# Scores of a chunked gated scan on four column tiles, collected compactly with one masked copy a level

## The chip, the core and the metric

The kernel runs on one core of a Trainium2 chip. The metric is the device time of one execution in microseconds; less is better. The profile comes from one execution. Its engines are called PE (TensorE, matmuls), PEld (the weight loads of TensorE, which overlap the matmuls), DVE (VectorE), ACT (ScalarE), POOL (GpSimd) and SP (SyncE, which issues the DMAs).

## What is computed

One layer of a trunk over 2048 latent positions of width 1024, with a prefix of 256 positions, all in float32. The input is normalised, modulated and projected (w_in); the projections feed a bidirectional gated scan with four heads of 128 channels and a spatial gate with four heads; then come an output projection and a gated MLP with a 3x3 convolution. The change is inside the scan's products within a chunk. In the reference they are:

```
b = jnp.cumsum(gc, axis=2)
diff = b[:, :, :, None, :] - b[:, :, None, :, :]
decay = jnp.where(mask, jnp.exp(jnp.where(mask, diff, 0.0)), 0.0)
scores = jnp.einsum('bhtk,bhsk,bhtsk->bhts', qc, kc, decay)
o = o_inter + jnp.einsum('bhts,bhsv->bhtv', scores, vc)
```

The score of a position t with a position s sums, over the 128 channels, q at t, k at s and the product of the forget gates between them. One such sum runs forwards in time and one backwards.

## The kernel before

The sequence is worked in two halves of 1024 positions (TH), a half in 8 chunks (NCH) of 128 positions (P). In the first stage, function run_banks sends the projections of all heads to PE, bank by bank: a bank is 512 positions of 128 output columns, 24 matmuls of 512 columns in a split precision (xh, xl and whi, wlo; tile pj, three banks). Into this stream two queues of generators put their steps: hg_q the scans of the heads, bg_q the background work (among it w_down_ops, line 1024). A step comes when the planner's clock T.t (class Tensor, line 57), which adds an assumed time for each matmul, has passed the wait that the last step yielded; the clock is looked at between the matmuls of a bank (slot). The wait counts from behind the matmuls of the step that yields it. Before the last four banks open_wo drains both queues.

A head's scan is the generator hg (line 795), which runs eight times: four heads in each of two halves. Layout: positions of a chunk by positions of a chunk, tile sc of 128 partitions (s) by 8 chunks by 128 (t). Its steps are:

- the diagonal: kd is q times the sum of both directions' k; its sums over the 128 channels are needed in every row, so a matmul with a matrix of ones takes them. kd is split in kh and kl (fp32r, an ACT cast at line 802 and a DVE subtraction at line 804), and column_sums (line 790) multiplies both by the 128 ones, 512 columns at a time. ACT copies the result over all of sc (line 813).
- level 1: the products kn of neighbours, split in knh and knl (lines 825, 826) and summed in the same way; a DVE masked copy puts them in sc (line 856).
- levels B = 2, 4, 8, 16, 32, 64 (LV): within a block of 2B positions, each half of B is scored against the other. For each chunk two float32 matmuls of 64 weights (from K) and 64 columns (from Q) fill two squares of 64 by 64, in two PSUM banks (tag sc, two of them); the two stand on different halves of the array's columns, since their outputs go to PSUM partitions 0 to 63 and 64 to 127. Up to level 32, four DVE masked copies (line 860) put in sc what belongs to the level; level 64 is copied by ACT (lines 852, 853).
- behind each level, Q is multiplied by the level's gate products (level_update, line 518), K likewise into another tile (level_keys: DVE and POOL at line 595, ACT copies at line 598, at level 64 lines 587 and 588), and the gate products are merged (next_tot, line 525). Then the step yields 4.2.
- behind the levels: K is transposed (kt), the states of the chunks are made and chained (fs and bs_, line 781), and sc, Q and the states give the output. The output gates (o_gate, line 771) run later.

On-chip tiles are named by tags; tiles of the same tag share their slots, and a new one waits until the old one was read for the last time. kd lies in Q, kh and sc in slot S, kl and knl in T1, knh in on. The slot fs holds the states and, in the second half, the gate sgb of the scan that was deferred. Except where pin stands, the framework may order the instructions of an engine anew.

Of the kernel before, what the change touches and what calls it, by code (L numbers as in the profile page):

```python
# [17 lines left out]

P = 128
HB = 64  # L20
D = 1024
NK = D // P
SEQ = 2048
# [28 lines left out]
def view(t, off, dims):  # L52

    return bass.AP(t.tensor, t.offset + off, [list(t.ap[0])] + [list(d) for d in dims])


class Tensor:
# [5 lines left out]
    def matmul(self, out, lhsT, rhs, **kw):  # L63
        n = 1
        for _, count in rhs.ap[1:]:
            n *= count
        m = lhsT.ap[-1][1] / P
        self.t += n / 2400 + 0.0135 if rhs.dtype == F32R else 2 * max(0.112 * m, n / 1200 + 0.005)
        return self.engine.matmul(out, lhsT, rhs, **kw)  # L69

    def transpose(self, out, in_, identity):
# [16 lines left out]
def tile_trunk(ctx, tc, x, c, cx, c_ctx, w_ada, b_ada, norm_mix, norm_ffn, w_in, hg_norm, sgu_g, sgu_b,  # L88
# [105 lines left out]
    with es1:  # L194
# [5 lines left out]
        wa = [p1.tile([P, NK, TH], F32, tag=t, name="wa", align_bytes=AL) for t in ("xl", "xh")]  # L200
        wsT = pm.tile([P, NH, P], F32, name="wsT")
        rh = pm.tile([P, NH, P], F32, name="rh")
        msk = pm.tile([P, 8, P], U8, name="msk")
        hf = [pm.tile([P, P], F32, name=f"hf{h}") for h in range(NH)]
        hb = [pm.tile([P, P], F32, name=f"hb{h}") for h in range(NH)]
        tb0 = [pm.tile([P, NCH], F32, name=f"tb0_{h}") for h in range(NH)]
# [1 line left out]
        def bank(tag):  # L208
            return ps.tile([P, 512], F32, tag=tag, name=tag, bufs={"pj": 3, "sc": 2, "mi": 3}[tag])
# [260 lines left out]
        def misc():  # L470

            for l in range(0, 8, 4):
                mf = pm.tile([P, 4, P], F32, tag="gu", name="mf", bufs=2)
                ld(mf, masks.rearrange("p (l j) -> p l j", j=P)[:, l:l + 4, :])
                V.tensor_copy(msk[:, l:l + 4, :], mf)
            yield 1.0
            wsr = pm.tile([P, NH, P], F32, tag="nt", name="wsr", bufs=2)
            ld(wsr, w_sp[0].rearrange("h p q -> p h q"))
            bsb = pm.tile([P, NH, P], F32, tag="nt", name="bsb", bufs=2)
            ld(bsb, b_sp[0:1].broadcast_to([P, NH, P]))  # L480
            yield 5.0
            pv = bank("mi")
            for h in range(NH):
                T.transpose(pv[:, h * P:(h + 1) * P], wsr[:, h, :], ident)
            V.tensor_copy(wsT, pv.rearrange("p (h q) -> p h q", q=P))
            yield 2.5
            pv = bank("mi")
            for h in range(NH):
                T.matmul(pv[:, h * P:(h + 1) * P], ones, wsT[:, h, :], start=True, stop=True)
            for h in range(NH):  # L490
                V.scalar_tensor_tensor(out=rh[:, h, :], in0=pv[:, h * P:(h + 1) * P], scalar=sgb[:, h:h + 1],
                                       in1=bsb[:, h, :], op0=ALU.mult, op1=ALU.add)
            yield 0.0
# [293 lines left out]
                    V.scalar_tensor_tensor(out=o, in0=states[:, i + 1, :], scalar=tot(i), in1=states[:, i, :],  # L787
                                           op0=ALU.mult, op1=ALU.add)

        def column_sums(to, hi, lo):  # L790

            T.matmul(to, ones_r, hi, start=True, stop=False)
            T.matmul(to, ones_r, lo, start=False, stop=True)

        def hg(hh, h, F, K, qs, vt, sgt):
            Q = ph.tile([P, 2, TH], F32, tag="Q", name="Q", align_bytes=AL)
            kd = Q[:, 0, :]
            V.tensor_add(kd, K[:, 0, :], K[:, 1, :])
            V.tensor_mul(kd, kd, qs)
            kh = ph.tile([P, TH], F32R, tag="S", name="kh")  # L800
            kl = ph.tile([P, TH], F32R, tag="T1", name="kl")
            S.copy(kh, kd)
            V.tensor_mul(Q[:, 1, :], qs, F[:, 1, :])
            V.tensor_sub(kl, kd, kh.bitcast(F32))
            V.tensor_mul(Q[:, 0, :], qs, F[:, 0, :])
            yield 6.5
            pbs = [bank("sc") for g in range(2)]
            for g in range(2):
                sl = slice(g * 512, g * 512 + 512)
                column_sums(pbs[g], kh[:, sl], kl[:, sl])  # L810
            sc = ph.tile([P, NCH, P], F32, tag="S", name="sc")
            for g in range(2):
                S.copy(sc[:, 4 * g:4 * g + 4, :], pbs[g].rearrange("p (c t) -> p c t", t=P))
            done.add((hh, h, "diag"))
            yield 1.6
            gates_done()
# [1 line left out]
            kn = K2[:, 0, :]  # L818
            V.tensor_mul(view(kn, 0, [[1, 2], [2, TH // 2]]), view(K, 1, [[-1, 2], [2, TH // 2]]),
                         view(Q, 0, [[TH + 1, 2], [2, TH // 2]]))  # L820
            knl = ph.tile([P, TH], F32R, tag="T1", name="knl")
            knh = [ph.tile([P, 512], F32R, tag="on", name="knh", bufs=2) for g in range(2)]
            for g in range(2):
                sl = slice(g * 512, g * 512 + 512)
                S.copy(knh[g], kn[:, sl])
                V.tensor_sub(knl[:, sl], kn[:, sl], knh[g].bitcast(F32))
            yield 3.2
            tot = F
            for l, B in enumerate(LV):
                pbs = [bank("sc") for g in range(2)]  # L830
                for g in range(0, NCH, 4):
                    pb = pbs[g // 4]
                    if B == 1:
                        column_sums(pb, knh[g // 4], knl[:, g * P:g * P + 512])
                    for i in range(4) if B > 1 else ():
                        for r in range(2):
                            off, e = (g + i) * P, r * HB
                            c = e if B < HB else HB - e
                            dims = [[2 * B, HB // (2 * B)], [TH + B, 2], [1, B]]
                            d = e  # L840
                            if B < 4:
                                dims = [[TH + B, 2], [2 * B, HB // (2 * B)], [1, B]]
                            if B == HB:
                                dims, d = [[1, B]], (TH + B) * (1 - r)
                            o = pb[e:e + HB, i * P + c:i * P + c + HB]
                            if B < 4:
                                o = view(o, 0, [[B, 2], [2 * B, HB // (2 * B)], [1, B]])
                            T.matmul(o, K[:, 0, off + e:off + e + HB], view(Q, off + d, dims), start=True, stop=True)
                for g in range(0, NCH, 4):
                    pq = pbs[g // 4].rearrange("p (c t) -> p c t", t=P)  # L850
                    if B == P // 2:
                        S.copy(sc[:B, g:g + 4, B:], pq[:B, :, B:])
                        S.copy(sc[B:, g:g + 4, :B], pq[B:, :, :B])
                        continue
                    if B == 1:
                        V.copy_predicated(sc[:, g:g + 4, :], view(msk, l * P, [[0, 4], [1, P]]), pq)
                        continue
                    for e in (0, HB):
                        q = slice(e, e + HB)
                        V.copy_predicated(sc[q, g:g + 4, q], view(msk[q], l * P + e, [[0, 4], [1, HB]]), pq[q, :, q])  # L860
                level_update(Q, TH, B, tot, False)
                K, K2 = level_keys(K, B, tot, K2), None
                tot = next_tot(tot, TH, B)
                yield 4.2
# [1034 lines left out]
```

## Time and profile before

| | us |
|---|---|
| median of three runs | 2421.59 (2420.18 to 2424.41) |
| the profiled execution | 2420.11 |
| its span, first to last instruction | 2418.3 |
| projections, first half's last part and scans, busy PE of 222 to 930 us | 689.9 of 708 |
| output projection's first matmul | 959.5 |

How to read the rows: a group has the line, the engine, the operation, out<-in by the program's names, then out<-in as partitions x elements and type, and xcount; behind it the busy time in us, the mean of one in ns, and the idle time of the engine just before them with what ended it. In the order of time a row has the start in us, the length in us and the same names; rows of the same kind that follow each other are merged under one xcount. A waits row has who waited for whom, then us in total, times, longest. Matmuls go through line 69 and transposes through line 73, so these are told apart by tiles. A float32 matmul is two records, one of fp32r is one. Lengths of matmuls overlap; their starts tell the pace.

### The profile page before, as it was taken

How to read it: one execution, taken by the hardware profiler on the slowest of the kernel's cores; microseconds unless marked ns; L12 is line 12 of the kernel's file. 1: busy time of each engine (PE TensorE's matmuls, PEld its weight loads, DVE VectorE, ACT ScalarE, POOL GpSimd, SP SyncE). 2: the span in 40 equal slices, each digit the busy share in tenths (PEclk: the TensorE clock that was granted, in tenths of full speed). 3: DMA queues.
4: the chain of work that ended last, by engine and by line, in shares of the span. 5: the costliest groups of instructions: out<-in, count | busy, mean ns of one | idle time of the engine just before them, and what ended most of it. 6: DMA issues, size and time to landing. Idle time of an engine off the chain costs nothing.

```text
span 2418.3 us, 33888 instructions
## 1 busy us (share of the span) xinstructions
PE 2376.4 (98%) x12479; PEld 1954.8 (81%) x12479; DVE 1671.6 (69%) x2331; ACT 1045.5 (43%) x1803; POOL 869.0 (36%) x788
## 2 busy tenths in 40 slices
PE   8999999999999999999999999999999999999998
PEld 5887778888888877888788888888888888888887
DVE  5757896766696795565696666648866773676876
ACT  3554434434444443444544344444444443332243
POOL 1021110110121122001788878788887870000002
PEclk9999999999999999999999999999999999999999
DMA  8365445463455325669732222652222239834745
GB/s 307 112 205 171 157 132 186 141 218 123 136 183 183 100 68 197 204 201 284 257 103 82 91 80 86 213 206 97 86 94 94 86 113 391 273 118 151 228 152 200
DMA packets 304052, 393.39 MB, mean 163 GB/s; under 512 B 32633, under 2 KB 215681, under 8 KB 300813
## 3 DMA queue, kind: packets, MB, share of 16 engines
q1 hardware_dynamic: 300596, 390.46, 48.1%
q8 instruction: 98, 1.61, 0.3%
q10 hardware_dynamic: 3289, 0.76, 0.1%
q14 instruction: 69, 0.57, 0.1%
HBM read 283.60 MB, written 107.55 MB: 162 GB/s over the span
## 4 chain that ended last, share of the span: by engine, by line
PE 49%; issue 2%; POOL 1%; DMA 1%; DVE 0%; ACT 0%; SPq 0%; POOLq 0%; ACTq 0%; DVEq 0%
PE ux L69 19%; PE dn L69 16%; PE uz L69 14%; DMA raw<-in_w_up_dram 1%; POOL rr L1759 0%; DMA yf<-yd 0%; POOL Al L137 0%; DMA xn<-cv 0%; POOL ra L1758 0%; POOL ra L1756 0%; DVE fl L137 0%; PE ux L73 0%; ACT jk L1747 0%; ACT yst L136 0%; POOL raw L1273 0%
## 5 line engine op out<-in xcount | busy, mean ns | idle before, releaser
L1464 DVE SCALAR_TENSOR_TENSOR dn<-gp,taps,dn 128x1024 f32<-128x1024 f32 x352 | 448.0, 1284 | 97.0 <-ACT dn L1461 92.6
L69 PE MATMUL dn<-thl,mhl 128*128 128x512 f32 x1680 | 381.0, 389 | 0.0
L69 PEld LDWEIGHTS dn<-thl,mhl 128*128 128x128 f32 x1680 | 315.3, 188 | 65.6 <-issue 0.2
L137 POOL TENSOR_TENSOR Al<-raw,Ah 128x512 fp32r<-128x512 f32 x264 | 341.2, 1308 | 73.5 <-ACT Ah L136 41.3
L69 PE MATMUL pj<-xh,whi 128*128 128x512 f32 x896 | 363.4, 406 | 0.0
L69 PE MATMUL pj<-xl,whi 128*128 128x512 f32 x896 | 353.6, 395 | 0.0
L69 PE MATMUL pj<-xh,wlo 128*128 128x512 f32 x896 | 351.8, 393 | 0.0
L136 ACT CAST Ah<-raw 128x512 fp32r<-128x512 f32 x264 | 163.1, 620 | 242.5 <-PE ux L69 129.3
L69 PE MATMUL ux<-xah,Ah 128*128 128x512 f32 x528 | 205.7, 390 | 0.3 <-ACT keep L1528 0.3
L69 PEld LDWEIGHTS pj<-xh,whi 128*128 128x128 f32 x896 | 168.9, 189 | 36.3 <-issue 3.5
L69 PEld LDWEIGHTS pj<-xh,wlo 128*128 128x128 f32 x896 | 168.9, 189 | 35.3
L69 PEld LDWEIGHTS pj<-xl,whi 128*128 128x128 f32 x896 | 169.3, 189 | 31.4 <-DVE xl L256 0.8
L69 PE MATMUL dn<-wo,o 128*128 128x512 f32 x768 | 182.4, 394 | 0.0
L69 PE MATMUL uz<-yf,Ah 128*128 128x512 f32 x704 | 174.0, 389 | 0.0
L595 POOL TENSOR_TENSOR K<-K,tot 128x512 f32<-128x512 f32 x40 | 63.1, 1579 | 295.5 <-DVE tot L525 163.8
L69 PEld LDWEIGHTS dn<-wo,o 128*128 128x128 f32 x768 | 142.1, 188 | 29.0
L69 PE MATMUL ux<-yf,Ah 128*128 128x512 f32 x528 | 155.4, 389 | 0.0
L69 PEld LDWEIGHTS uz<-yf,Ah 128*128 128x128 f32 x704 | 132.1, 188 | 27.4
L69 PE MATMUL ux<-xah,Al 128*128 128x512 f32 x528 | 141.8, 390 | 1.1 <-POOL Al L137 1.1
L69 PE MATMUL ux<-xal,Ah 128*128 128x512 f32 x352 | 137.1, 389 | 0.0
L137 DVE TENSOR_TENSOR wlo<-raw,whi 128x1024 fp32r<-128x1024 f32 x67 | 84.0, 1253 | 70.6 <-ACT whi L136 67.8
L1756 POOL TENSOR_SCALAR ra<-ss 128x1 f32<-128x1 f32 x8 | 3.2, 396 | 359.6 <-ACT jk L1747 359.6
(345 smaller groups left out, 4376.7 us busy)
## 6 DMA issues: line engine op xcount, KB each, us to landing
raw<-in_w_up_dram SPq DMA_DIRECT2D x88, 512.0 KB, 3.4
mr<-m SPq DMA_DIRECT2D x85, 512.0 KB, 5.2
raw<-in_w_in_dram SPq DMA_DIRECT2D x68, 512.0 KB, 4.3
sT<-wd SPq DMA_DIRECT2D x88, 256.0 KB, 5.1
raw<-in_w_ada_dram SPq DMA_DIRECT2D x32, 512.0 KB, 4.3
yf<-yd SPq DMA_DIRECT2D x14, 1024.0 KB, 9.8
m<-cv SPq DMA_DIRECT2D x22, 544.0 KB, 2.7
raw<-in_w_down_dram SPq DMA_DIRECT2D x22, 512.0 KB, 4.2
```

The lines of the kernel that those rows point to most:

```text
L69: return self.engine.matmul(out, lhsT, rhs, **kw)
L136: keep(S.copy(hi, raw))
L137: (eng or G).tensor_sub(lo, raw, hi.bitcast(F32))
L595: e.tensor_mul(view(K2, row * W + o, src), view(K, o, src), view(tot, t0, [[4, n], [ts, 2], [0, B]]))
L1464: V.scalar_tensor_tensor(out=cr, in0=gt[:, t // 3:t // 3 + RH, t % 3:t % 3 + GW], scalar=taps[:, t * NF + f:t * NF + f + 1], in1=cr, op0=A ...
L1756: G.tensor_scalar(out=a, in0=ss, scalar1=plus, scalar2=None, op0=ALU.add)
```

## The change

- Level 1's and the diagonal's sums take float32 inputs as they are: no split. column_sums makes four products with 32 columns of ones (QB = 32), one for each quarter of the output partitions; quarter e takes columns e to e+31 of each chunk. kd gets a tile of its own in slot S.
- The scores of the diagonal and of levels up to 16 are kept compactly in near, 128 partitions by 8 chunks by 32: a position's own block of 32 alone. near lies in slot fs. ACT copies the diagonal there; one DVE masked copy of 128x256 for each level 1, 2, 4, 8 and 16 adds the level. The mask tile shrinks to 32 columns and is cast in eight pieces.
- Levels 2 to 32 run four float32 matmuls a chunk, of 32 weights and 32 columns, into one PSUM bank; level 64 keeps two of 64 by 64, now in one bank as well.
- At level 32 ACT lays near out in sc with four copies of 32x256 and copies that level's scores with four more; at level 64 it copies 64x512 twice.
- The planner's time for a float32 matmul is now multiplied by its share of the array's columns.

```diff
@@ -18,6 +18,7 @@
 
 P = 128
 HB = 64
+QB = 32
 D = 1024
 NK = D // P
 SEQ = 2048
@@ -65,7 +66,7 @@
         for _, count in rhs.ap[1:]:
             n *= count
         m = lhsT.ap[-1][1] / P
-        self.t += n / 2400 + 0.0135 if rhs.dtype == F32R else 2 * max(0.112 * m, n / 1200 + 0.005)
+        self.t += n / 2400 + 0.0135 if rhs.dtype == F32R else 2 * m * max(0.112 * m, n / 1200 + 0.005)
         return self.engine.matmul(out, lhsT, rhs, **kw)
 
     def transpose(self, out, in_, identity):
@@ -200,7 +201,7 @@
         wa = [p1.tile([P, NK, TH], F32, tag=t, name="wa", align_bytes=AL) for t in ("xl", "xh")]
         wsT = pm.tile([P, NH, P], F32, name="wsT")
         rh = pm.tile([P, NH, P], F32, name="rh")
-        msk = pm.tile([P, 8, P], U8, name="msk")
+        msk = pm.tile([P, 8, QB], U8, name="msk")
         hf = [pm.tile([P, P], F32, name=f"hf{h}") for h in range(NH)]
         hb = [pm.tile([P, P], F32, name=f"hb{h}") for h in range(NH)]
         tb0 = [pm.tile([P, NCH], F32, name=f"tb0_{h}") for h in range(NH)]
@@ -472,7 +473,8 @@
             for l in range(0, 8, 4):
                 mf = pm.tile([P, 4, P], F32, tag="gu", name="mf", bufs=2)
                 ld(mf, masks.rearrange("p (l j) -> p l j", j=P)[:, l:l + 4, :])
-                V.tensor_copy(msk[:, l:l + 4, :], mf)
+                for e in range(0, P, QB):
+                    V.tensor_copy(msk[e:e + QB, l:l + 4, :], mf[e:e + QB, :, e:e + QB])
             yield 1.0
             wsr = pm.tile([P, NH, P], F32, tag="nt", name="wsr", bufs=2)
             ld(wsr, w_sp[0].rearrange("h p q -> p h q"))
@@ -787,30 +789,25 @@
                     V.scalar_tensor_tensor(out=o, in0=states[:, i + 1, :], scalar=tot(i), in1=states[:, i, :],
                                            op0=ALU.mult, op1=ALU.add)
 
-        def column_sums(to, hi, lo):
-
-            T.matmul(to, ones_r, hi, start=True, stop=False)
-            T.matmul(to, ones_r, lo, start=False, stop=True)
+        def column_sums(to, prod):
+
+            for e in range(0, P, QB):
+                T.matmul(view(to[e:e + QB], 0, [[QB, NCH], [1, QB]]), ones[:, :QB],
+                         view(prod, e, [[P, NCH], [1, QB]]), start=True, stop=True)
 
         def hg(hh, h, F, K, qs, vt, sgt):
             Q = ph.tile([P, 2, TH], F32, tag="Q", name="Q", align_bytes=AL)
-            kd = Q[:, 0, :]
+            kd = ph.tile([P, TH], F32, tag="S", name="kd")
             V.tensor_add(kd, K[:, 0, :], K[:, 1, :])
             V.tensor_mul(kd, kd, qs)
-            kh = ph.tile([P, TH], F32R, tag="S", name="kh")
-            kl = ph.tile([P, TH], F32R, tag="T1", name="kl")
-            S.copy(kh, kd)
             V.tensor_mul(Q[:, 1, :], qs, F[:, 1, :])
-            V.tensor_sub(kl, kd, kh.bitcast(F32))
             V.tensor_mul(Q[:, 0, :], qs, F[:, 0, :])
             yield 6.5
-            pbs = [bank("sc") for g in range(2)]
-            for g in range(2):
-                sl = slice(g * 512, g * 512 + 512)
-                column_sums(pbs[g], kh[:, sl], kl[:, sl])
-            sc = ph.tile([P, NCH, P], F32, tag="S", name="sc")
-            for g in range(2):
-                S.copy(sc[:, 4 * g:4 * g + 4, :], pbs[g].rearrange("p (c t) -> p c t", t=P))
+            pb = bank("sc")
+            column_sums(pb, kd)
+            near = ph.tile([P, NCH + 1, P], F32, tag="fs", name="fs")[:, :2, :]
+            near = near.rearrange("p c (u t) -> p (c u) t", t=QB)
+            S.copy(near, pb[:, :NCH * QB].rearrange("p (c t) -> p c t", t=QB))
             done.add((hh, h, "diag"))
             yield 1.6
             gates_done()
@@ -818,46 +815,35 @@
             kn = K2[:, 0, :]
             V.tensor_mul(view(kn, 0, [[1, 2], [2, TH // 2]]), view(K, 1, [[-1, 2], [2, TH // 2]]),
                          view(Q, 0, [[TH + 1, 2], [2, TH // 2]]))
-            knl = ph.tile([P, TH], F32R, tag="T1", name="knl")
-            knh = [ph.tile([P, 512], F32R, tag="on", name="knh", bufs=2) for g in range(2)]
-            for g in range(2):
-                sl = slice(g * 512, g * 512 + 512)
-                S.copy(knh[g], kn[:, sl])
-                V.tensor_sub(knl[:, sl], kn[:, sl], knh[g].bitcast(F32))
             yield 3.2
             tot = F
             for l, B in enumerate(LV):
-                pbs = [bank("sc") for g in range(2)]
-                for g in range(0, NCH, 4):
-                    pb = pbs[g // 4]
-                    if B == 1:
-                        column_sums(pb, knh[g // 4], knl[:, g * P:g * P + 512])
-                    for i in range(4) if B > 1 else ():
-                        for r in range(2):
-                            off, e = (g + i) * P, r * HB
-                            c = e if B < HB else HB - e
-                            dims = [[2 * B, HB // (2 * B)], [TH + B, 2], [1, B]]
-                            d = e
-                            if B < 4:
-                                dims = [[TH + B, 2], [2 * B, HB // (2 * B)], [1, B]]
-                            if B == HB:
-                                dims, d = [[1, B]], (TH + B) * (1 - r)
-                            o = pb[e:e + HB, i * P + c:i * P + c + HB]
-                            if B < 4:
-                                o = view(o, 0, [[B, 2], [2 * B, HB // (2 * B)], [1, B]])
-                            T.matmul(o, K[:, 0, off + e:off + e + HB], view(Q, off + d, dims), start=True, stop=True)
-                for g in range(0, NCH, 4):
-                    pq = pbs[g // 4].rearrange("p (c t) -> p c t", t=P)
-                    if B == P // 2:
-                        S.copy(sc[:B, g:g + 4, B:], pq[:B, :, B:])
-                        S.copy(sc[B:, g:g + 4, :B], pq[B:, :, :B])
-                        continue
-                    if B == 1:
-                        V.copy_predicated(sc[:, g:g + 4, :], view(msk, l * P, [[0, 4], [1, P]]), pq)
-                        continue
-                    for e in (0, HB):
-                        q = slice(e, e + HB)
-                        V.copy_predicated(sc[q, g:g + 4, q], view(msk[q], l * P + e, [[0, 4], [1, HB]]), pq[q, :, q])
+                pb = bank("sc")
+                M = max(QB, B)
+                pq = pb[:, :NCH * M].rearrange("p (c t) -> p c t", t=M)
+                if B == 1:
+                    column_sums(pb, kn)
+                for i in range(NCH) if B > 1 else ():
+                    for e in range(0, P, M):
+                        o, q = pq[e:e + M, i, :], i * P + e
+                        d = [[2 * B, M // (2 * B)], [TH + B, 2], [1, B]]
+                        if B < 4:
+                            o = view(o, 0, [[B, 2], [2 * B, M // (2 * B)], [1, B]])
+                            d = [d[1], d[0], d[2]]
+                        if B >= QB:
+                            d, q = [[1, B]], i * P + (e if e & B else TH + e + B) - (e & B)
+                        T.matmul(o, K[:, 0, i * P + e:i * P + e + M], view(Q, q, d), start=True, stop=True)
+                if B < QB:
+                    V.copy_predicated(near, view(msk, l * QB, [[0, NCH], [1, QB]]), pq)
+                if B == QB:
+                    sc = ph.tile([P, NCH, P], F32, tag="S", name="sc")
+                    for e in range(0, P, QB):
+                        q = slice(e, e + QB)
+                        S.copy(sc[q, :, q], near[q])
+                if B >= QB:
+                    for e in range(0, P, B):
+                        q = slice(e, e + B)
+                        S.copy(sc[q, :, e ^ B:(e ^ B) + B], pq[q])
                 level_update(Q, TH, B, tot, False)
                 K, K2 = level_keys(K, B, tot, K2), None
                 tot = next_tot(tot, TH, B)
```

## The prediction

> **What bounds the kernel now.** I read the page first, then a table of stages, then the order of time inside one level of the scan.
>
> ```profile
> span 2418.3 us, 33888 instructions
> PE 2376.4 (98%) x12479; PEld 1954.8 (81%) x12479; DVE 1671.6 (69%) x2331; ACT 1045.5 (43%) x1803; POOL 869.0 (36%) x788
> ```
>
> ```profile
> 222.00:930.00 708.00, 689.92 (x4756) 571.81 (x4755) 538.21 (x873) 302.55 (x570) 114.86 (x100) 1.00 0.44 147
> ```
>
> The second is a row of the table of stages; after the length stand the busy times of PE, PEld, DVE, ACT and POOL. The eight heads' scans (function hg) run between 222 and 930 us. PE is busy for 690 of those 708 us, at a granted clock of 1.00, and DVE for 538, with ACT and POOL far behind. So PE's stream is the clock of this stage: a microsecond that a level takes out of it comes off the end, whereas DVE or ACT time counts only where PE waits for it. How long PE waits for these matmuls is read from the waits of PE in the scan's stretch:
>
> ```profile
> PE sc L69 <- DVE Q L518: 3.8, 2, 2.5
> PE sc L69 <- DVE K L595: 3.3, 5, 1.0
> ...
> PE sc L69 <- DVE tot L525: 1.3, 3, 0.5
> PE sc L69 <- ACT whi L136: 1.1, 1, 1.1
> ...
> PE sc L69 <- DVE kl L804: 0.8, 1, 0.8
> ```
>
> Together 10.3 us. That bounds what lighter DVE work alone can give. The rest must come from the matmuls themselves, so I look at one level in order of time (start, length, then the instruction):
>
> ```profile
> 428.26 0.39 PE L69 MATMUL pj<-xh,whi 128*128 128x512 f32 x1
> 428.49 0.39 PE L69 MATMUL pj<-xl,whi 128*128 128x512 f32 x1
> 428.71 0.39 PE L69 MATMUL pj<-xh,wlo 128*128 128x512 f32 x1
> 429.03 1.15 PE L69 MATMUL sc<-Q,K 128*64 128x64 f32 x32
> 430.11 0.50 PE L69 MATMUL pj<-xh,whi 128*128 128x512 f32 x1
> 430.45 0.39 PE L69 MATMUL pj<-xl,whi 128*128 128x512 f32 x1
> ```
>
> Starts count, not lengths, because matmuls overlap. Projections start 0.23 us apart. Going into the level the step is 0.32 (0.09 more), the level takes 1.08 to the next projection start, and the step after that is 0.34 (0.11 more). The 16 float32 products of a level are 32 records, two passes each.
>
> **How the two column tiles run today.** This decides the forecast.
>
> ```profile
> L69 PE MATMUL sc<-Q,K 128*64 128x64 f32 x1536 | 55.9, 226 | 9.8 <-DVE Q L518 3.8 <-DVE K L595 3.3 <-DVE tot L525 1.3
> ...
> 429.03 0.28 PE L69 MATMUL sc<-Q,K 128*64 128x64 f32 x2
> ...
> 279.77 3.95 PE L69 MATMUL mi<-vt,kt 128*128 128x128 f32 x32
> 283.48 0.48 PE L69 MATMUL pj<-xh,whi 128*128 128x512 f32 x1
> ...
> 232.15 1.02 PE L69 MATMUL mi<-acc,ones_r 128*1 128x512 f32 x2
> ...
> L69 PE MATMUL mi<-acc,ones_r 128*1 128x512 f32 x6 | 3.1, 591 | 0.0
> ```
>
> One record lasts 0.22, so first and last start of a level lie 1.15 - 0.22 = 0.93 apart: 31 steps of 0.030. A full-width float32 record of 128 columns takes (283.48 - 279.77)/32 = 0.116, so 64 columns alone would take 0.058. At 0.030 two records go at once, one in each half of the array. The second row shows it directly: asked only for the first 0.05 us of the level, the timeline has two matmuls started, which together take 0.28. So a tile's turn is 0.058 for 64 columns, and two tiles run side by side. What is left of 1.08 after 0.93 is 0.15 until the projection starts, of which one turn, 0.06, is the last record and 0.09 the switch out.
>
> **The change on PE.** Levels 2 to 32 turn from 32 records on two tiles into 64 records of 32 weights and 32 columns on four. If the turn goes on following the columns (0.029) and four tiles run at once, there are again 16 turns, each half as long: 0.93 becomes 0.465 and the tail 0.15 becomes 0.12. That is 0.49 less a level. Five levels by eight heads make 40: **-19.6 us**. Level 64 keeps its 32 records.
>
> Column sums: each head has eight fp32r matmuls of 512 columns at a projection's pace, 8 x 0.23 = 1.8 us. They become two float32 sums, each of four products and eight records of 256 columns. Two such records of 512 columns start 1.02 - 0.59 = 0.43 apart (0.59 is the mean of one, 591 ns in the listing by line), so 256 columns take 0.215. Four tiles at once make two turns, 0.43, and the sum now also pays the switch, 0.09 + 0.09 + 0.11: 0.72 a sum, 1.44 a head. Saved 0.37 by 8: **-3.0 us**.
>
> **The change on DVE and ACT.** From the listing by line, same stretch:
>
> ```profile
> L860 DVE COPY_PREDICATED sc<-msk,sc 64x256 f32<-64x256 uint8 x160 | 71.4, 446 | 7.5 <-PE sc L69 4.7
> ...
> L598 ACT COPY K<-K 128x512 f32<-128x512 f32 x96 | 56.6, 638 | 85.2 <-DVE K L595 42.4 <-PE sc L69 20.5 <-POOL K L595 11.3
> ...
> L856 DVE COPY_PREDICATED sc<-msk,sc 128x512 f32<-128x512 uint8 x16 | 11.0, 726 | 0.2 <-PE sc L69 0.2
> ...
> L826 DVE TENSOR_TENSOR knl<-K,knh 128x512 fp32r<-128x512 f32 x16 | 10.3, 684 | 0.0
> ...
> L804 DVE TENSOR_TENSOR kl<-Q,kh 128x1024 fp32r<-128x1024 f32 x8 | 9.8, 1222 | 3.4 <-ACT kh L802 3.3
> ...
> L825 ACT CAST knh<-K 128x512 fp32r<-128x512 f32 x16 | 9.2, 624 | 8.6 <-DVE K L819 8.6
> ...
> L813 ACT COPY sc<-sc 128x512 f32<-128x512 f32 x16 | 8.6, 590 | 15.9 <-PE sc L69 15.9
> ...
> L802 ACT CAST kh<-Q 128x1024 fp32r<-128x1024 f32 x8 | 8.4, 1049 | 13.6 <-DVE Q L799 13.3
> ...
> L853 ACT COPY sc<-sc 64x256 f32<-64x256 f32 x16 | 5.9, 368 | 0.2
> ...
> L852 ACT COPY sc<-sc 64x256 f32<-64x256 f32 x16 | 5.8, 365 | 11.5 <-PE sc L69 11.4
> ```
>
> DVE loses its four groups (71.4 + 11.0 + 10.3 + 9.8 = 102.5 us) and gets 40 masked copies of 128x256. That shape isn't shown; between 446 ns (64x256) and 726 (128x512) I take 446, the row with its number of columns, so 17.8 us. Net -85 us, about an eighth of the stage. As PE covers it, it counts only in waits. A level's DVE queue before the updates of Q and K is 3 x 0.45 = 1.3 us shorter. Of the 10.3 us of waits I take 5 as gone; the rest has casts and background work in front of it, which stay. One wait is worth more than itself:
>
> ```profile
> 808.27 1.68 PE L69 MATMUL sc<-Q,K 128*64 128x64 f32 x32 [2.47 <-DVE Q L518]
> 809.88 0.80 PE L69 MATMUL pj<-xh,whi 128*128 128x512 f32 x1
> 810.48 0.63 PE L69 MATMUL pj<-xl,whi 128*128 128x512 f32 x1
> 810.90 0.63 PE L69 MATMUL pj<-xh,wlo 128*128 128x512 f32 x1
> ```
>
> After 2.47 us idle the level takes 0.53 more and projections go 0.42 apart for some steps: some 2 us that go with this wait. Waits: **-7 us** (0 to -13).
>
> ACT loses 8.4 + 8.6 + 9.2 + 5.8 + 5.9 = 37.9 us, 4.7 a head, and gets the copy of the diagonal to near, eight copies of 32x256 to lay out sc, and two of 64x512: by columns (365 for 256, 590 for 512) at most 9 x 0.37 + 2 x 0.59 = 4.5 a head. The sum is even, but the place moves: the eight copies (2.9 us) stand in level 32, ahead of or among the copies of K that level 64 needs (two of 0.64).
>
> ```profile
> 435.62 1.15 PE L69 MATMUL sc<-Q,K 128*64 128x64 f32 x32
> 441.68 1.15 PE L69 MATMUL sc<-Q,K 128*64 128x64 f32 x32
> ```
>
> Levels start 6.06 apart; without the level itself that leaves 4.9 us for 2.9 + 1.3 = 4.2. It fits, unless a cast or an activation falls between; then level 64 is late and the projections queue behind it on PE. Four of the eight read near alone and can go before. Bounds 0 and 1 us a head; I take 0.25: **+2 us**.
>
> near shares its slot with the last head's output gates in the second half, so the copy to near can wait there while ACT's queue stands behind it. Today's chain copy waits for the same release:
>
> ```profile
>   ACT fs L778: 3.5, 2
> ```
>
> That is ACT behind the gate's L771, 3.5 us in two waits, without a PE wait to its name; projections have three banks of 24 x 0.23 = 5.4 us each. I cost it at nothing. Without that cover it would be the same 3.5 us.
>
> The matmul planner counts less, by its formula, for each score product (a level 1.87 us before, 0.51 after; a head some 13.0 and 4.3), while the spacing of levels in projections stays, since a step's wait is counted from behind its own matmuls. Background work comes up to 7 x 8.7 = 61 us later:
>
> ```profile
> L1024 DVE TENSOR_TENSOR raw<-raw,g x22: 1212/1218/2311, 559.9 to 803.4; 128x1024 f32<-128x1024 f32 x22
> ...
> L69 PE MATMUL dn<-wo,o x768: 387/389/486, 959.5 to 1148.7; 128*128 128x512 f32 x192
> ```
>
> Its last piece, at 803, would come by 865. The drain stands four projection banks (22 us) before the output projection, at 937. No cost. The mask is cast in eight pieces in place of two around 59 us: under 1 us, neglected.
>
> **Sum.** -19.6 - 3.0 - 7 + 2 = -27.6. The profiled execution took 2420.1 us (span 2418.3), the median shown is 1.5 above it, so 2420.1 - 27.6 + 1.5 = **2394**. Its own range: without relief and with 8 us of ACT waits 2407; with all waits gone 2382.
>
> **Rivals.** *The stream is the limit.* A projection streams 512 columns in 0.23 and two tiles stream 128 in 0.058: both 2.2 columns a nanosecond. If that is all that the array is fed, four tiles take 128 columns in 0.058 too and a level stays at 0.93, since 64 x 32 columns are as many as 32 x 64. For it: the two numbers agree. Against it: each also follows from the turn of one tile. A sum is then 2048/2.2 = 0.93 + 0.29 = 1.22, or 2.44 a head, +5 in all; with 5 us of waits gone it cancels: 2421.
>
> *The issue of records is the limit*, and this one ends slower. A level has 64 instructions, loads and matmuls, in 0.93: 14.5 ns each, and no row here shows closer over so many. If 14.5 is what the queue can do, 128 instructions take 1.86: +0.90 a level (its tail is 0.03 shorter), +36, less 3 and 5: 2450. It decides from 18 ns a record on: with 8 us saved elsewhere, 40 levels may each lose 0.20, so 64 records may take 1.16. Against it: two starts lie inside the first 0.05 us, and 0.058 is just half of the full-width record, so tiles bound today's pace and the queue only has to be no slower. For it: the number of records doubles, and nothing here tests the queue beyond.
>
> The Trainium skill speaks for this rival in "TensorE: Matmul & The Clock Gate", section "Wait — 56ns, not 53.3ns?": start to start never drops below about 25 ns, however few columns; by that rule a level would be 64 x 25 ns = 1.6 plus 0.21, an estimate of +0.64 a level and 2439 in all. Its section "Packing small matmuls — row/col tiling" has different tiles start some 4 ns apart; by that the forecast stands, and the two starts inside 0.05 us side with this one.
>
> *Part of the new layout is late:* forecast for PE, but level 64 waits 1 us in each head and nothing is relieved: 2407. It lies in the forecast's own range.
>
> **Chances.** Forecast 0.55 (late layout included), stream 0.20, issue 0.25. Two tiles side by side are shown, four are not; hence no more than 0.55. 80% asks for the forecast's range, all of the stream's case and the lower part of issue's: 2380 to 2440. A measurement here tells about 0.2%, 4.8 us, from no change. Faster: 0.55 and a quarter of the stream's case, 0.60; same 0.15; slower 0.25.
>
> **What would show it.** In order of time a level should read x64 and some 0.7 long, with 0.6 to the next projection; 1.15 means the stream, 1.6 or more the issue. A sum should read x8 and under 0.7. The masked copies should be 40 of about 0.45. Waits of PE for DVE at sc should halve, and the level 64 matmuls should not wait for ACT. The forecast is wrong if four tiles don't run at once, or if a switch into four tiles costs much more than the 0.09 and 0.2 seen with two.

## The result, and the profile after

| | before | after |
|---|---|---|
| median, us | 2421.08 | 2383.57 (2381.78 to 2386.29) |
| ratio, after to before | | 0.9844, interval 0.9826 to 0.9861 |
| profiled execution, us | 2420.11 | 2384.07 |
| its span, us | 2418.3 | 2382.3 |
| output projection's first matmul, us | 959.5 | 924.6 |

The kernel is 37.5 us faster in the medians. Of the 36.0 us between the two spans, 34.9 are there when the output projection starts. The page of the changed kernel and its table of stages (after the length: PE, PEld, DVE, ACT, POOL busy):

```profile
span 2382.3 us, 36421 instructions
...
PE 2353.0 (99%) x13823; PEld 1926.6 (81%) x13823; DVE 1610.4 (68%) x2177; ACT 1044.8 (44%) x1819; POOL 878.1 (37%) x788
```

```profile
222.00:905.00 683.00, 676.01 (x6145) 552.30 (x6145) 478.35 (x724) 305.92 (x605) 125.41 (x104) 1.00 0.46 155
```

The scans begin at the same time (their first sums start at 222.6 us, before at 223.2), and their last products with sc start 35 us earlier, at 894.5 in place of 929.4. In the stretch to 905 us PE is idle for 7.0 us; in the one to 930 us of the kernel before it was 18.1. PE has 1344 records more and is busy for less time. One level in order of time shows how:

```profile
426.33 0.39 PE L70 MATMUL pj<-xh,whi 128*128 128x512 f32 x1
426.55 0.39 PE L70 MATMUL pj<-xl,whi 128*128 128x512 f32 x1
426.78 0.39 PE L70 MATMUL pj<-xh,wlo 128*128 128x512 f32 x1
427.10 0.76 PE L70 MATMUL sc<-Q,K 128*32 128x32 f32 x64
427.79 0.51 PE L70 MATMUL pj<-xh,whi 128*128 128x512 f32 x1
428.13 0.39 PE L70 MATMUL pj<-xl,whi 128*128 128x512 f32 x1
```

Into the level 0.32 and behind it 0.34, as before; the level itself takes 0.69 to the next projection where it took 1.08. And a column sum:

```profile
398.35 0.39 PE L70 MATMUL pj<-xh,wlo 128*128 128x512 f32 x1
398.67 0.64 PE L70 MATMUL sc<-kd,ones_r 128*32 128x256 f32 x8
399.24 0.50 PE L70 MATMUL pj<-xh,whi 128*128 128x512 f32 x1
399.57 0.39 PE L70 MATMUL pj<-xl,whi 128*128 128x512 f32 x1
```

Eight records of 256 columns take 0.57 to the next start; one after the other, at the prediction's 0.215 each, they would take 1.7. The groups by line that answer to those of before:

```profile
L846 ACT COPY sc<-sc 32x256 f32<-32x256 f32 (+1 forms) x48 | 21.0, 437 | 14.2 <-PE sc L70 13.7
...
L837 DVE COPY_PREDICATED fs<-msk,sc 128x256 f32<-128x256 uint8 x40 | 17.8, 446 | 15.8 <-PE sc L70 11.7 <-ACT sig L1017 3.9
...
L842 ACT COPY sc<-fs 32x256 f32<-32x256 f32 x32 | 12.9, 403 | 1.8 <-DVE fs L837 1.4
...
L810 ACT COPY fs<-sc 128x256 f32<-128x256 f32 x8 | 3.0, 374 | 19.1 <-DVE ot L773 8.9 <-PE sc L70 8.2 <-DVE sgt L1018 2.0
```

And the waits of PE (total, times, longest); these are all of the scans' stretch over 0.3 us:

```profile
PE mi L74 <- ACT kt L860: 2.4, 3, 1.9
PE mi L74 <- DVE on L743: 1.9, 3, 1.0
PE sc L70 <- DVE Q L520: 1.7, 3, 0.9
PE mi L70 <- DVE bs__8839 L789: 0.6, 1, 0.6
PE mi L70 <- issue: 0.5, 1, 0.5
PE mi L70 <- DVE fs L783: 0.4, 1, 0.4
PE mi L74 <- DVE nt L723: 0.4, 1, 0.4
```

Of the 10.3 us that PE waited at sc, 1.7 are left. No wait at sc is for ACT.

One thing on DVE got slower. One level after the change, then one before it, in order of time:

```profile
427.90 0.45 DVE L837 COPY_PREDICATED fs<-msk,sc 128x256 f32<-128x256 uint8 x1 [0.87 <-PE sc L70]
...
428.10 1.09 POOL L597 TENSOR_TENSOR K<-K,tot 128x512 f32<-128x512 f32 x1 [4.55 <-PE sc L70]
...
428.24 2.02 DVE L520 TENSOR_TENSOR Q<-Q,tot 128x1024 f32<-128x1024 f32 x1
```

```profile
430.43 1.41 POOL L595 TENSOR_TENSOR K<-K,tot 128x512 f32<-128x512 f32 x1 [3.61 <-PE sc L69]
...
430.85 1.82 DVE L860 COPY_PREDICATED sc<-msk,sc 64x256 f32<-64x256 uint8 x4
...
432.68 1.22 DVE L518 TENSOR_TENSOR Q<-Q,tot 128x1024 f32<-128x1024 f32 x1
```

With one masked copy in front of it in place of four, the update of Q runs while POOL multiplies K, and takes 2.02 us in place of 1.22. Of the 56 updates of Q after, 25 ran beside POOL's work, and each of these 25 was slow (2.04 on average, against 1.22 for the other 31). Before, two were slow.

To see where the time went I added up, over each of the two traces, the steps from a matmul's start to the next one's, sorted by the matmul that the step follows, up to the output projection:

| steps after | before, us | after, us | difference |
|---|---|---|---|
| scores of levels 2 to 64 | 52.6 | 36.7 | -15.9 |
| column sums | 17.3 | 9.1 | -8.2 |
| projections (their waits and the way into a burst included) | 659.5 | 651.1 | -8.4 |
| everything else (the rest of the 959.5 and 924.6) | 230.1 | 227.7 | -2.4 |

The projections' line holds the 16 new ways into a sum and back (0.09 + 0.11 each, 3.2 us in all), so some 11.6 us of waits and slow projections went. A part of the slow projections is the clock: in the trace before, the granted clock is 0.50 for 3.4 us from 808.7 us and again from 911.1, and in the trace after once in the scans, from 448.1. At half the clock 3.4 us lose an estimated 1.7, so one stretch less is some 2 of the 11.6.

### The profile page after: what moved, and what is told of

It is laid out like the page before. It is cut to its first block, busy times and chain, and to the rows that moved or that the text cites. A ratio compares the mean times of both kernels' runs of the same rounds, so it can differ in the third digit from the quotient of the medians.

```text
span 2382.3 us, 36421 instructions
## 1 busy us (share of the span) xinstructions
PE 2353.0 (99%) x13823; PEld 1926.6 (81%) x13823; DVE 1610.4 (68%) x2177; ACT 1044.8 (44%) x1819; POOL 878.1 (37%) x788
## 4 chain that ended last, share of the span: by engine, by line
PE 48%; issue 2%; POOL 1%; DVE 0%; ACT 0%; DMA 0%; POOLq 0%; SPq 0%; ACTq 0%
PE ux L70 19%; PE dn L70 15%; PE uz L70 14%; POOL rr L1745 0%; DMA raw<-in_w_up_dram 0%; POOL Al L138 0%; POOL ra L1744 0%; POOL ra L1742 0%; ACT jk L1733 0%; POOL raw L1259 0%; DVE odd L85 0%; POOL raw L1257 0%; POOL s L1255 0%; POOL fl L1255 0%; DVE dn L1450 0%
```

## The experiments

The theory: the gain has two sources that add up, PE's own shorter bursts (levels and sums) and waits that went because DVE has less to do. Rivals: the bursts alone or DVE alone pay, or the planner's new formula does, by moving background work.

**tiles_only**: the kernel before with the scores of levels 2 to 32 on four tiles.

```diff
-                            T.matmul(o, K[:, 0, off + e:off + e + HB], view(Q, off + d, dims), start=True, stop=True)
+                few = 1 < B < HB
...
+                for i in range(NCH) if few else ():
+                    for e in range(0, P, 32):
...
+                        T.matmul(o, K[:, 0, i * P + e:i * P + e + 32], view(Q, q, d), start=True, stop=True)
+                for e in range(0, P, 32) if few else ():
+                    q, c = slice(e, e + 32), e ^ (B & 32)
+                    V.copy_predicated(sc[q, :, c:c + 32], view(msk[q], l * P + c, [[0, NCH], [1, 32]]), pq[q])
```

> The kernel before with nothing but the scores of levels 2 to 32 on four tiles of 32; sums split in fp32r as before, four masked copies a level as before (of 32x256 instead of 64x256), the planner's formula as before. Theory A (PE's own stream pays): a level takes 0.39 us less on PE, 40 levels, so some 16 us less than before: 2405 (2400 to 2409), with PE's waits for DVE at sc still near 10 us. Rival (DVE's relief pays, a shorter burst is refilled with waiting): DVE has as many copies as before, so 2414 or more, with waits at sc above 15 us.

Measured: 2408.67, ratio 0.9946 (0.9929 to 0.9963), 13 us less than before. In the range of the theory, but short of 16, and the waits say where the rest may have gone (tiles_only, waits of PE in the scans):

```profile
PE sc L69 <- DVE Q L518: 6.5, 9, 1.7
PE sc L69 <- DVE K L595: 5.1, 5, 1.5
...
PE sc L69 <- DVE tot L525: 2.3, 4, 1.0
```

These three were 8.4 us before and are 13.9 here. With two smaller ones the waits at sc come to 15.8 us, where the theory expected near 10 and the rival over 15: the time is the theory's, the waits are the rival's. PE arrives earlier, DVE doesn't, and a part of the gain turns into waiting.

**two_tiles** and **half_tiles** undo the tiles in the changed kernel. In two_tiles M is 64 for the levels up to 32; in half_tiles the records stay and, at levels 2 to 16, go to half as many tiles. Both leave out a part of the scores, so they serve for the time alone. The edit of half_tiles:

```diff
+                        if B <= 16:
+                            r = e % HB
+                            o = pq[r:r + M, i, :]
```

> The changed kernel with the scores of levels 2 to 32 as products of 64 weights and 64 columns on two tiles, 32 records a level as before the change; all else as changed, one masked copy a level (which takes the first 32 columns of each square, so the scores of every second quarter are left out up to level 16). Theory A (PE's stream): 40 levels of 0.39 us, 13 to 17 us slower than the changed kernel, 2397 to 2401. Rival (the shorter burst is refilled with waiting, as in tiles_only, so the longer one costs little): 2386 to 2394.

> The changed kernel with the products of levels 2 to 16 of the third and fourth quarter sent to the first and second tile (the lower half of the scores is left out there): 64 records as changed, but on two tiles. If a tile's own turn of 33 ns sets the pace: 32 turns for 16, a level 0.5 us longer, 32 levels, 2397 to 2402. If the issue of records sets it (8.3 ns a record): no change, 2381 to 2387.

Measured: two_tiles 2397.22, ratio 0.9905 (0.9889 to 0.9922), 13.6 us over the changed kernel's median; half_tiles 2394.55 (two executions), ratio 0.9893 (0.9872 to 0.9915), 11 over it. The first hit; the second came under its range of 2397 to 2402, but its level shows which limit holds (half_tiles, order of time):

```profile
417.17 0.39 PE L70 MATMUL pj<-xh,wlo 128*128 128x512 f32 x1
417.49 1.21 PE L70 MATMUL sc<-Q,K 128*32 128x32 f32 x64
418.62 0.50 PE L70 MATMUL pj<-xh,whi 128*128 128x512 f32 x1
```

The same 64 records take 1.13 to the next projection on two tiles and 0.69 on four. So the pace is the tile's turn, not the issue of records: with 0.2 for one record, 1.01 us are 32 turns of 0.032, and on four tiles 0.56 are 16 turns of 0.035. The starts themselves agree: on two tiles a pair of starts comes every 32 ns; on four, in the first half of this level, four starts come every 32 ns, about 7 ns apart.

**sums_only** and **sums_idle_split**: the kernel before with the new sums, without and with the instructions of the old split.

```diff
-            T.matmul(to, ones_r, hi, start=True, stop=False)
-            T.matmul(to, ones_r, lo, start=False, stop=True)
+            for e in range(0, P, 32):
+                T.matmul(view(to[e:e + 32], 0, [[32, NCH], [1, 32]]), ones[:, :32],
+                         view(prod, e, [[P, NCH], [1, 32]]), start=True, stop=True)
...
-            S.copy(kh, kd)
-            V.tensor_sub(kl, kd, kh.bitcast(F32))
```

> The kernel before with nothing but the sums of the diagonal and of level 1 in float32 on four tiles of 32 (no split; four copies of 32x256 by ACT for the diagonal and four masked copies of 32x256 for level 1). Theory A: the sums' own stream gives 5 us (17.3 us for their 64 records before, 16 x 0.77 after) and the waits for the split another 1 to 3: 2414 (2410 to 2417). Rival (the switches into four tiles eat the gain): 2419 to 2422.

> sums_only with the casts and subtractions of the split kept beside the new sums (their results are read by nothing), so that DVE and ACT have the work of before and PE the float32 sums on four tiles. If sums_only's 14 us are PE's stream and the split's own wait (5 to 8 us) and the rest is DVE relief: 2412 to 2417. If all of it is PE's: 2405 to 2410. If all of it is DVE's and ACT's relief: 2418 or more.

Measured: sums_only 2407.28, ratio 0.9943 (0.9928 to 0.9957), 14 us less, better than the 4 to 11 us expected; sums_idle_split 2414.88, ratio 0.9984 (0.9975 to 0.9994), 4 us less by the ratio. So only some 4 us (1 to 6 by the interval) are PE's own sums. The other 10 or so are the split's work, 20 us of DVE and 18 us of ACT. With its results unused, but its instructions kept beside the new sums, PE waits again (sums_idle_split; this execution took 2420.05, 5 us above the median, so its waits may be larger than most):

```profile
PE sc L69 <- DVE K L595: 7.2, 10, 2.2
PE sc L69 <- DVE Q L518: 4.5, 7, 1.0
```

**four_copies**: the changed kernel with the one masked copy cut into four.

```diff
-                    V.copy_predicated(near, view(msk, l * QB, [[0, NCH], [1, QB]]), pq)
+                    for e in range(0, P, QB):
+                        q = slice(e, e + QB)
+                        V.copy_predicated(near[q], view(msk[q], l * QB, [[0, NCH], [1, QB]]), pq[q])
```

> The changed kernel with the one masked copy of 128x256 of levels 1 to 16 cut into four of 32x256, as many as before: DVE has some 53 us more to do, PE's instructions are the same. Theory A (a part of the gain, some 12 us, is waits that lighter DVE work took away): 5 to 9 us slower than the changed kernel, 2389 to 2393, with PE's waits for DVE at sc back from 1.7 to 5 us or more. Rival (the waits went for another reason, the planner or the unsplit sums): 2382 to 2386.

Measured: 2393.45, ratio 0.9883 (0.9868 to 0.9897), 9.9 us over the changed kernel, with all of its matmuls, just above the 5 to 9 expected. One wait has most of the loss (four_copies):

```profile
PE sc L70 <- DVE Q L520: 10.5, 13, 2.0
```

It was 1.7 in the changed kernel. The update of Q stands in DVE's order behind the masked copies, and three copies more of 0.45 make it late for the next level. DVE's busy time grew by 37.4 us only (from 1610.4 to 1647.9), though the 120 copies more are 53: only one update of Q ran beside POOL's work here, and the others took 1.22 us again. DVE's share of the span says nothing of the wait.

**planner_old** and **planner_alone**: the formula's factor m taken out of the changed kernel, and put into the kernel before.

```diff
-2 * m * max(0.112 * m, n / 1200 + 0.005)
+2 * max(0.112 * m, n / 1200 + 0.005)
```

> The changed kernel with the planner's formula for a float32 matmul as before (without the share of the columns), so that the background work comes earlier again. Theory A (the planner's formula pays nothing): 2381 to 2387, like the changed kernel. Rival (the background work was moved away from the scans, and that took the waits): 2390 or more.

> The kernel before with the planner's new formula alone, so that a level of 64-wide products counts 0.93 planned us in place of 1.87 and background work comes later; no instruction is added or removed. If the formula pays by itself what planner_old lost (some 6 us): 2413 to 2417. If what planner_old lost hangs on where a few background steps fall beside the new, shorter levels: within 3 us of the kernel before, either side.

Measured: planner_old 2390.12, ratio 0.9871 (0.9856 to 0.9886); planner_alone 2417.46, ratio 0.9991 (0.9982 to 1.0). I had expected nothing of the first and it came at the rival's number: 6.5 us over the changed kernel's median, though the two intervals just meet. planner_alone takes 2 us off the kernel before (0 to 4). The trace of planner_old has two large new waits. The larger (order of time, what ended an idle time in brackets):

```profile
401.56 0.69 DVE L992 TENSOR_TENSOR raw<-raw,g 128x512 f32<-128x512 f32 x1 [3.86 <-DMA raw<-in_w_out_dram]
...
402.17 1.22 DVE L138 TENSOR_TENSOR wlo<-raw,whi 128x1024 fp32r<-128x1024 f32 x1
...
403.30 1.22 DVE L801 TENSOR_TENSOR kd<-K 128x1024 f32<-128x1024 f32 x1
...
405.57 1.22 DVE L802 TENSOR_TENSOR kd<-kd,qs 128x1024 f32<-128x1024 f32 x1
...
406.84 0.64 PE L70 MATMUL sc<-kd,ones_r 128*32 128x256 f32 x8 [2.91 <-DVE kd L802]
```

DVE waits 3.86 us for a background load, and what PE needs, kd, stands behind it. With the old formula a burst of 0.7 us counts 2.0 planned us, and this step falls just there. The second wait, 2.03 us at 427.8 for ACT's copy of vv (line 606), has the same line in front of it: DVE waits 2.04 us for its load, and two casts of ACT stand ahead of the copy. In the changed kernel the same step falls elsewhere, and costs there too: its longest wait of PE, 1.9 us for kt at 447.7, comes behind 3.29 us in which DVE waits at line 992. Not all of the 6.5 us need be the formula's: in the trace of planner_old the granted clock is 0.50 for 6.8 us from 81 us on, ahead of the scans, an estimated 3.4 us that the changed kernel's trace doesn't have. planner_alone stayed within the 3 us of its second reading, so the formula alone doesn't pay what planner_old lost. What was left was a matter of place: I then gave that step more time.

**later_loads**, **one_sum_step**, **both**, with **after_again** beside them: a longer planned wait for the load (8.0 to 11.0), and the diagonal's sums put directly before level 1's.

```diff
-                    yield 8.0
+                    yield 11.0
```

> The changed kernel once more, to compare the next three with it on the same chip: 2381 to 2387.

> The changed kernel with the background step of w_out 11.0 planned us behind its load in place of 8.0, so that the load has landed when DVE comes to it. Theory (a background multiplication that waits for its load at the head of DVE's queue holds up what PE waits for): DVE's 23.5 us of idle time in front of that line fall under 10, the 2.1 us wait of PE for the transposed keys goes with them, and the kernel takes 2 to 5 us less than the changed one. Rival (these waits of DVE lie where nothing of PE's is queued): within 1 us of it.

> The changed kernel with the diagonal's sums put directly before those of level 1, in one step, so that PE goes into the four-tile form and back once less in each head. Theory (each way there and back costs 0.26 us beside the records): 2 us less than the changed kernel. Rival (the copy of the diagonal to near now stands in front of the first masked copy and makes level 2 late): the same or up to 4 us more.

> The two edits of later_loads and one_sum_step together. Theory: 4 to 7 us less than the changed kernel. Rival: no less than the better of the two alone.

| run | median, us | ratio to before | interval |
|---|---|---|---|
| after_again | 2383.96 | 0.9847 | 0.9832 to 0.9862 |
| later_loads | 2387.08 | 0.9864 | 0.9848 to 0.9881 |
| one_sum_step | 2382.58 | 0.9845 | 0.9831 to 0.9860 |
| both | 2386.41 | 0.9856 | 0.9842 to 0.9871 |

None is better than the changed kernel beyond its interval; later_loads was expected to save 2 to 5 us and both 4 to 7. DVE's idle time at that line didn't fall but rose (later_loads, groups by line):

```profile
L992 DVE TENSOR_TENSOR raw<-raw,g 128x512 f32<-128x512 f32 x16 | 11.2, 709 | 31.4 <-DMA raw<-in_w_out_dram 22.7 <-DMA g<-g_d 5.7 <-issue 3.0
```

It is 23.5 us in the changed kernel and 14.8 in the one before, the slowest of the three. So this idle time isn't a measure of loss, and a longer planned wait doesn't cure it. The wait that it was to take away did go (PE for kt, from 2.4 us to 0.5), but others came: 2.2 us for K (line 597) and 1.7 for nt (line 723). Why the idle time rises stays open. one_sum_step leaves out eight ways into a burst and back, some 2 us; it came 1.4 under after_again, less than its interval can tell.

## Why the prediction held

Forecast 2394 in a range of 2380 to 2440, measured 2383.57. The mechanism was right for PE, with the relief of DVE sized too small: 27.6 us forecast, 37.5 found. The experiments add up to nearly that: 13 for the tiles, 4 for the sums, 10 for the split, 10 for the masked copies. That the measured time lies inside the range is in part luck. With the sum's own best terms (waits -13, ACT 0) the time is 2421.6 - 19.6 - 3.0 - 13 = 2386, not the 2382 written, and the measured time is below that.

- **Scores on four tiles, -19.6: too large.** Four tiles run at once, as it took them to; the steps show -15.9. The turn was mis-sized: I halved 0.058 to 0.029, but half_tiles shows 0.032 and the changed level, over its whole length, 0.035. From 128 columns to 64 the turn had halved (0.116 to 0.058); from 64 to 32 it fell by a little less. Why is not shown. In the kernel's time the tiles are worth 13 (tiles_only) to 13.6 us (two_tiles).
- **Column sums, -3.0: nearly right.** sums_idle_split shows 4 us. A sum costs 0.09 + 0.57 + 0.10 = 0.76 with its ways in and out; 0.72 was forecast. The old sums were also dearer than the 1.84 us a head put down: 17.3/8 = 2.16.
- **DVE's relief, -7: too small.** This is where the surplus comes from. The copies were exact (40 of 446 ns), but DVE's busy time fell by 61 us over the span (1671.6 to 1610.4), where 85 were forecast, mostly since 25 updates of Q became slow beside POOL, 20 us in all. Even so more waiting went than forecast: I let only 5 of the 10.3 us of waits go, and 8.6 went. The prediction's claim that 10.3 us bounds what lighter DVE work can give was wrong: four_copies loses 9.9 us by 120 copies, and the split, by sums_only against sums_idle_split, some 10 more. I had counted only waits at sc in the trace before, but PE waits for DVE more often once its own bursts are shorter (tiles_only), and a wait can cost more than its length. The wait of 2.47 us at 808.27 that the prediction showed is such a case: the slow steps behind it are the clock, granted at 0.50 from 808.7 to 812.1 us. That each copy fewer lets the next level's Q come earlier fits the wait of four_copies; how the 20 us divide into waits and slow steps is not shown.
- **ACT's new place in level 32, +2: not seen.** No wait of PE at sc is for ACT. L810 waits 8.9 us for the gates in slot fs, and nothing waits for L810: the cover held.
- **The planner, 0: open.** planner_old lost 6.5 us, of which two waits of 2.9 and 2.0 are shown and some 3.4 may be the clock; planner_alone gained 2. I had looked only at whether the background work still ends in time, not at what it meets on the way. How much of the 37.5 us is due to where background steps happen to fall is not settled.
- **The rivals.** The stream as limit fell: 64 records of 32 columns in 0.56 us are 3.7 columns a nanosecond, above the 2.2 at which it would have stood. The issue of records fell with half_tiles, where the same 64 records take 1.01 us on two tiles; on four, 64 records in 0.56 us are 9 ns each, while it would have decided from 18. The late layout wasn't seen. The Trainium skill's 25 ns from start to start ("TensorE: Matmul & The Clock Gate", "Wait — 56ns, not 53.3ns?") doesn't bind across column tiles here; the 4 ns from tile to tile of its section "Part 3: Packing small matmuls — row/col tiling" leaves room for the 9 ns found.

## What to carry to other kernels

Where two tiles of the array are seen to run side by side, the turn of one tile is the number to measure; splitting further paid nearly by the columns here: 58 ns for 64 columns, 32 for 32. When PE sets the end, ask of each edit on another engine not how much busy time it removes but what stands behind it in that engine's order: 120 copies more on an engine busy for two thirds of the time cost 10 us. Ask also what an instruction that moves forward will run beside: the updates of Q lost to POOL 20 us of what the copies had freed. Bursts that get shorter ask for their operands earlier: the tiles alone gave 13 of the 16 us that their own steps saved. That a lighter DVE brings back the rest is not shown: in the changed kernel the tiles are worth 13.6 us by the medians and 15 by the ratios (two_tiles), and the intervals are wider than these differences.

## What the runs showed of the hardware

Matmuls of 32 weights and 32 columns on four column tiles keep 64 weight loads and 64 matmuls flowing at 9 ns a pair, and the pace is set by the turn of a tile, 32 to 35 ns. A way into such a form and back costs a projection's pace 0.09 before, and 0.11 after it, the same for two tiles and four. A masked copy's time went by columns and not by partitions: 444 ns for 32x256 (four_copies), 446 for 64x256 and for 128x256, 726 for 128x512. The same copy took 448 ns beside POOL's product of K and 446 without it (before), while a DVE product of 128x1024 took 2.04 us beside POOL's work and 1.22 without it. The granted clock fell to 0.50 for 3.4 us at a time, and projections then started 0.42 apart in place of 0.23. The three times that it did so in the scans of the two kernels, it was within 0.5 us of PE's start after a wait of 1.9 to 2.5 us; the 2.9 us wait of planner_old was not followed by one.
